# Layer 0's projections: two sequences without a zero column between them, token mixing in instructions of 640 columns, all of it on VectorE

## The chip, the cores and the metric

The kernel runs on one core of a Trainium2 chip. The metric is the device time of one execution in microseconds (us). Five engines work side by side, each on its own list of instructions, in order: TensorE (PE for its products, PEld for its loading of stationary operands), VectorE (DVE), ScalarE (ACT), GpSimd (POOL) and SyncE (SP), which here only starts transfers. They wait for each other through semaphores.

## The reference, cut to what matters

One step of a trunk of two layers runs over 512 latent tokens and 128 context tokens, 1024 features each. Layer 0 mixes tokens with a recurrence in both directions. Its inputs come from a token shift:

```python
def centred_token_shift(x):
    zero = jnp.zeros_like(x[:, :1])
    prev = jnp.concatenate([zero, x[:, :-1]], axis=1)
    nxt = jnp.concatenate([x[:, 1:], zero], axis=1)
    return 0.5 * (prev + nxt)

delta = centred_token_shift(h) - h                      # h: modulated norm of x
xs = h[None] + delta[None] * mu[:, None, None, :]       # six mixed inputs
r, k, v = xs[0] @ w_r, xs[1] @ w_k, xs[2] @ w_v         # xs[3..5]: low-rank maps w, a, g
```

Neither sequence sees the other one: the first and the last token of each have a zero as their missing neighbour. The recurrence (the scan), the projection back, an MLP, layer 1's attention and its MLP follow.

## The kernel before, in words

Features lie on the 128 partitions, in 8 tiles (k = 0 to 7), and tokens along the columns: 512 latent, then 128 context, 640 in all. Products are made exact in float32 by splitting each factor into a rounded part and a rest, `xh` and `xl` for an input, `whi` and `wlo` for weights, and by three products of each pair of tiles, in two halves of 320 columns (`fm_step`, L205).

`start_norm` makes the modulated norm. `xt` is x divided by its rms (L434); `hp` (L447, ScalarE) is scale and shift of it, 644 columns wide: a zero, 512 latent columns, two zeros, 128 context columns, a zero. `n_s` (L450) is the sum of both neighbours of each column in one instruction of 642 columns, and `dl` (L452) is half of it less `hp`, one instruction for each sequence. The odd tiles of L434 and the even tiles of L450 run on GpSimd.

`phase_proj` makes the six mixed inputs. `mix(m, k)` writes a tile `mixt` of 640 columns with two instructions on VectorE (L477, 512 and 128 columns, since `hp` has zeros between the sequences) and hands it to `split`: ScalarE rounds it to `xh` (L247), and the rest `xl` (L248) is made on GpSimd, for k = 0 and 4 on VectorE. That is 48 mixes, 36 of them with `xl` on GpSimd. Two `mixt` buffers turn, 8 buffers hold `xh` and `xl` of an input that a whole product reads, and two more those of a low-rank step.

The order of the phase: the low-rank map of the decay (m = 3), with its second stage (`l2lo` L539, `l2x` L533, products L548 and L550, ScalarE L553); the mixes of m = 1, then for eight pieces the product of k and one step of the next low-rank map (m = 4); the mixes of m = 0, then for eight pieces the product of r, a step of the last map (m = 5) and all that r, k and a give, written to DRAM (L601 to L622; GpSimd adds and multiplies in L623 and L624); the mixes of m = 2 beside the gate (`l2x` L646 and L647, product, L652 and L653). Then v's product and the scan start, whose first loads are queued behind the last of these steps.

The program is written in this order, and a scheduler at build time, which works from estimated costs, sets the order on each engine. A change of instructions in one place can so shift others, in later phases too.

Of the kernel before, what the change touches and what calls it, by code (L numbers as in the profile page):

```python
# [28 lines left out]
# ---------------------------------------------------------------- host layout  # L29
# [16 lines left out]
def _constants():  # L46
# [18 lines left out]
    # masks of the chunk products: rows (b | k), columns (at | rt), one per direction  # L65
# [43 lines left out]
def _tmaj(v):  # L109
    """[1024] of (ph, pp, hp, v) -> [(hp, pp, t), (ph, v)]"""  # L110
    a = np.asarray(v).reshape(4, 2, 2, 64).transpose(2, 1, 0, 3).reshape(4, 1, 256)
    return np.broadcast_to(a, (4, 32, 256)).reshape(P, 256)


def _bias(rpb):
    """Relative position bias of every query against its key band, -1e30 outside of the window:
    [head, query (g, r, j), kind of column block, key (g, r, j)]."""
# [54 lines left out]
# ---------------------------------------------------------------- device  # L172
class K:
# [11 lines left out]
    # -- weights: 128 columns of a [1024, n] matrix -> exact float32r pair  # L185
# [10 lines left out]
    # -- feature-major product of one 128-column piece: two PSUM tiles [128, 320]  # L196
# [3 lines left out]
    def fm_step(self, ps, w, x, k, n):  # L200
        """Columns 0 .. 319 and the others: tokens and whatever columns follow them."""
        N = x[0].shape[-1]
        for j, (a, b) in enumerate(((w[0], x[0]), (w[0], x[1]), (w[1], x[0]))):
            for g, (c, e) in enumerate(((0, HALF), (HALF, N))):
                self.nc.tensor.matmul(ps[g][:, :e - c], lhsT=a[:, k, :], rhs=b[:, c:e],  # L205
                                      start=(k == 0 and j == 0), stop=(k == n - 1 and j == 2))
# [7 lines left out]
    # -- token-major product, 256 columns at a time; out(t, b, psum)  # L214
# [36 lines left out]
    # -- y = x ** -0.5 on VectorE  # L251
# [14 lines left out]
    # -- adaLN vectors  # L266
# [12 lines left out]
    def ada_first(self, l, blk, pool, pa, mm=None):  # L279
        """Columns 256 * blk .. + 256 of layer l's adaLN, summed over four rows each."""  # L280
# [11 lines left out]
    def ada_second(self, l, blk, sb, pm, mm=None):  # L292
        """... and on into mods[l][:, 2 * blk : 2 * blk + 2, :]."""
# [8 lines left out]
    def gscale(self, l, s, pool):  # L302
        """norm_g * (1 + scale) -> [128, 8, 2]"""
# [21 lines left out]
    # -- 1/rms of every token, on all partitions: [128, 640]  # L325
# [14 lines left out]
    def ssq(self, k):  # L340
        """Feature tile k of the residual is complete: its squares into the running sum."""
# [8 lines left out]
    def rms_first(self, acc, pool):  # L350
        """-> 1/rms, token-major."""
# [12 lines left out]
    def rms_second(self, rs, pool):  # L364
        """... on all partitions."""
# [13 lines left out]
    # ------------------------------------------------------------------  # L379
    def run(self):  # L380
        nc, tc = self.nc, self.tc
        with ExitStack() as st:
# [6 lines left out]
            # per 128 tokens and four head pairs: kk, r; per direction kd, bp; decay exponents  # L389
# [28 lines left out]
    def start_norm(self, st, hp, dl):  # L418
        """hp: modulated norm of x with a zero around each sequence; dl: what the token shift adds."""
# [10 lines left out]
        nc.vector.memset(hp[:, :, 513:515], 0.0)  # L430
        nc.vector.memset(hp[:, :, 643:644], 0.0)
        rb = self.rms_bcast(xt, p2)
        for k in range(KT):
            (nc.gpsimd if k % 2 else nc.vector).tensor_tensor(xt[:, k, :], xt[:, k, :], rb, op=ALU.mult)  # L434
        gs = self.const.tile([P, 8, 2], F32, name="gs00")
        m = self.mods[0]
        for j in range(4):
# [7 lines left out]
            for k in range(2 * j, 2 * j + 2):  # L445
                for o, a, c, i in ((1, 0, TS, 0), (515, TS, TP, 1)):
                    nc.scalar.activation(hp[:, k, o:o + c], xt[:, k, a:a + c], AF.Identity, scale=gs[:, k, i:i + 1],  # L447
                                         bias=m[:, k, i:i + 1])
                s = p2.tile([P, 642], F32, name="n_s")
                (nc.vector if k % 2 else nc.gpsimd).tensor_tensor(s, hp[:, k, 0:642], hp[:, k, 2:644], op=ALU.add)  # L450
                for (a, b, c) in ((0, 0, TS), (TS, 514, TP)):
                    nc.vector.scalar_tensor_tensor(dl[:, k, a:a + c], s[:, b:b + c], 0.5,  # L452
                                                   hp[:, k, b + 1:b + 1 + c], op0=ALU.mult, op1=ALU.subtract)

    def phase_proj(self, sc):
        nc, tc = self.nc, self.tc
        with ExitStack() as st:
# [5 lines left out]
            hp = hpool.tile([P, KT, 644], F32, name="hp")  # L463
# [10 lines left out]
            def mix(m, k):  # L474
                t = mp.tile([P, T], F32, name="mixt")
                for (a, b, c) in ((0, 1, TS), (TS, 515, TP)):
                    nc.vector.scalar_tensor_tensor(t[:, a:a + c], dl[:, k, a:a + c], mu[:, m * 8 + k:m * 8 + k + 1],  # L477
                                                   hp[:, k, b:b + c], op0=ALU.mult, op1=ALU.add)
                return self.split(xq if m != 2 and k % 4 == 3 else xp, t, lo_eng=nc.gpsimd if k % 4 else nc.vector)
# [23 lines left out]
            class Lora1:  # L503
                """First stage of a low-rank map, one feature tile at a time."""
# [20 lines left out]
            def lora2(lw, j):  # L525
                """Second stage of the low-rank maps: stacked exact pairs."""
# [39 lines left out]
            # k and the decay exponents  # L566
# [21 lines left out]
            # r, and all that r, k and a give  # L588
# [55 lines left out]
            # gate  # L644
# [13 lines left out]
            # v, token-major, while the scan's first step is prepared  # L658
# [12 lines left out]
    # -- sums over the features of every head: [32 * (token tile) + head, token], the prompt's in columns 128 .. 255  # L671
# [14 lines left out]
    def head_tokens(self, y, psm):  # L686
        """... token-major: [token, 32 * (token tile) + head]."""
# [5 lines left out]
    def head_bcast(self, pool, y):  # L693
        """What a product needs to bring per-head factors to all features: rows twice, exact pair."""
# [14 lines left out]
    # ------------------------------------------------------------------  # L709
    def c_slots(self, pool, n, par):  # L710
        """Tiles of a window: [16 (z, e, q), at | rt], half identities, [8 (e, q), b | k time-major]."""
# [5 lines left out]
    def scan_pools(self, st):  # L717
# [9 lines left out]
        # state and chunk values [z, pp, ph, v]: head half z has G on partition half z, (U | V) on the other  # L727
# [4 lines left out]
        # window tiles of even and odd steps  # L732
# [99 lines left out]
    def mm(self, *a, op=None, **k):  # L832
        """Matmul issued behind the previous one of this kind."""
# [15 lines left out]
    def start_sample(self, d):  # L849
        """The given state into the next tile of direction d."""  # L850
# [14 lines left out]
    def fill(self, n):  # L865
        """Emit up to n groups of chunk products of coming units, as far as there is room."""
# [15 lines left out]
    def prep_elem(self, ts, hg, d, i):  # L882
        """Decays of a unit (four head pairs, one direction, a window of 64 tokens) and the scaled r, k, kk, b."""
# [47 lines left out]
    def prep_group(self, ts, hg, d, i, e):  # L931
        """Chunk products and time-major copies, eight (head, chunk) at a time."""
# [28 lines left out]
    def invert(self, ts):  # L961
        """(I - N)^-1 of all 32x32 blocks of a step in place, one block per partition."""
# [20 lines left out]
    def chain_step(self, ts, n, e, d):  # L983
        """One chunk of one direction in four stages: R, U, state, Y."""
# [7 lines left out]
        if n == 1 and e == 0:  # L992
            # the tile that holds the prompt's last state is written out, the sample starts in the other one
# [63 lines left out]
    def state_update(self, ts, n, e, d, gu, nx, C):  # L1057
        """G of the next chunk: accumulated in PSUM within a window, copied to the tile of the next chunk."""
# [6 lines left out]
        if e == 0 and n < 2:  # L1065
            # a new window: its first G is in SBUF only
# [29 lines left out]
    def post_half(self, tt, hb, on_dve):  # L1096
        """Group norm, bonus and gate of 64 tokens; o goes out feature-major."""
# [52 lines left out]
    def residual(self, out, k, ps, gate, x):  # L1150
        """out = x + gate * product, for feature tile k (both PSUM tiles)."""
# [5 lines left out]
    def late_pools(self):  # L1157
        """The odd steps' tiles make room for the output projection."""
# [411 lines left out]
```

## Time and profile before

| | us |
|---|---|
| median of three runs (2279.73 to 2282.37) | 2279.94 |
| span of the profiled execution, first to last instruction | 2277.6 |
| PE busy in the span | 2022.0 |
| PEld / DVE / ACT / POOL busy | 1836.7 / 1198.3 / 866.0 / 544.3 |

The page gives no time of the profiled execution besides its span; the median of the runs is 2.3 us above it. The page cuts the span into 40 slices of 57 us. In the first 6 slices, in which layer 0's projections lie (from about 28 to 322 us), PE is busy for 5 to 9 tenths with the granted clock at 5 to 9 tenths of full speed, and DVE for 6 to 8 tenths. From slice 17 on PE is busy for 9 tenths and more at full clock. A share of busy time is an average over stretches with different limits; it is read by stretch.

### The profile page before, as it was taken

The numbers are of one execution on the slowest core, as the hardware profiler recorded it, in microseconds if no ns is written. First come the engines' busy times: TensorE is split into PE (matmuls) and PEld (weight loads), VectorE is DVE, ScalarE is ACT, GpSimd is POOL, SyncE is SP. The second block draws the span as 40 slices with busy tenths as digits, with TensorE's granted clock in tenths as the row PEclk, the third lists the DMA queues.
The fourth block names the chain that finished last, engine by engine and source line by source line (L and its number), as shares of the span: only waits on it lengthen the run. The fifth ranks groups of instructions, "written<-read, shape, count | busy, mean of one in ns | idle before, by whom it ended". The sixth has DMA issues, their size and how long they took to land.

```text
span 2277.6 us, 44909 instructions
## 1 busy us (share of the span) xinstructions
PE 2022.0 (89%) x18516; PEld 1836.7 (81%) x18516; DVE 1198.3 (53%) x2593; ACT 866.0 (38%) x1734; POOL 544.3 (24%) x602
## 2 busy tenths in 40 slices
PE   5898978875567567999999999999999999999999
PEld 2687867754456457899999999888777999999999
DVE  6838574676886865433333335334566643434342
ACT  3435454355454334322232233222476431313130
POOL 2404368465552143101010010000132110101010
PEclk8597979988788788899999999999899999999999
DMA  6344855454443454322222323443411232222221
GB/s 229 103 131 131 252 186 163 127 165 141 139 138 117 106 165 136 122 93 93 93 86 91 93 75 94 142 129 94 138 43 32 78 120 75 75 75 75 75 75 73
DMA packets 161388, 260.01 MB, mean 114 GB/s; under 512 B 46880, under 2 KB 103328, under 8 KB 161184
## 3 DMA queue, kind: packets, MB, share of 16 engines
q1 hardware_dynamic: 146816, 240.37, 33.9%
q10 hardware_dynamic: 14368, 16.78, 2.2%
q8 instruction: 145, 2.38, 0.4%
q14 instruction: 59, 0.48, 0.1%
HBM read 218.18 MB, written 37.35 MB: 112 GB/s over the span
## 4 chain that ended last, share of the span: by engine, by line
PE 64%; DVE 11%; DMA 4%; POOL 3%; ACT 2%; issue 2%; SPq 1%; ACTq 0%; DVEq 0%; POOLq 0%
PE psl L205 48%; PE psl L239 3%; DVE invX L978 2%; PE ps L1497 2%; DVE invT L975 2%; POOL C L929 2%; PE po L1534 2%; PE pp L834 2%; PE pt L1522 2%; DVE C L959 1%; PE pp L1201 1%; PE psl L286 1%; PE A L834 1%; DMA ld_s<-scr 1%; PE psl L1238 1%
## 5 line engine op out<-in xcount | busy, mean ns | idle before, releaser
L191 ACT CAST whi<-wraw 128x1024 fp32r<-128x1024 f32 x179 | 187.2, 1048 | 727.6 <-PE psl L205 696.3
L205 PE MATMUL psl<-xh,whi 128*128 128x320 f32 (+1 forms) x1712 | 422.4, 320 | 20.1 <-ACT whi L191 14.5
L205 PE MATMUL psl<-xl,whi 128*128 128x320 f32 (+1 forms) x1712 | 419.1, 318 | 10.3 <-POOL xl L248 5.4
L205 PE MATMUL psl<-xh,wlo 128*128 128x320 f32 (+1 forms) x1712 | 415.7, 316 | 2.2 <-DVE wlo L193 2.2
L205 PEld LDWEIGHTS psl<-xh,whi 128*128 128x128 f32 x1712 | 297.2, 193 | 40.8 <-ACT whi L191 18.8
L205 PEld LDWEIGHTS psl<-xl,whi 128*128 128x128 f32 x1712 | 297.4, 193 | 18.2 <-POOL xl L248 7.5
L205 PEld LDWEIGHTS psl<-xh,wlo 128*128 128x128 f32 x1712 | 298.6, 193 | 4.6 <-DVE wlo L193 2.6
L1317 POOL TENSOR_TENSOR relu<-relu 128x640 f32<-128x640 f32 x64 | 80.6, 1261 | 753.5 <-ACT relu L1316 748.8
L1154 DVE SCALAR_TENSOR_TENSOR xres<-psl,mods,xres 128x320 f32<-128x320 f32 (+2 forms) x216 | 81.7, 434 | 305.5 <-PE psl L205 305.5
L205 PE MATMUL psl<-hhh,wlo 128*128 128x320 f32 x1024 | 233.4, 309 | 0.0
L205 PE MATMUL psl<-hhl,whi 128*128 128x320 f32 x1024 | 233.3, 309 | 0.0
L205 PE MATMUL psl<-hhh,whi 128*128 128x320 f32 x1024 | 233.2, 309 | 0.0
L193 DVE TENSOR_TENSOR wlo<-wraw,whi 128x1024 fp32r<-128x1024 f32 x179 | 222.6, 1246 | 9.6 <-ACT whi L191 9.2
L205 PEld LDWEIGHTS psl<-hhh,whi 128*128 128x128 f32 x1024 | 171.2, 188 | 0.4 <-issue 0.4
L205 PEld LDWEIGHTS psl<-hhh,wlo 128*128 128x128 f32 x1024 | 171.2, 188 | 0.0
L205 PEld LDWEIGHTS psl<-hhl,whi 128*128 128x128 f32 x1024 | 171.1, 188 | 0.0
L834 PE MATMUL pp<-C,KB 128*64 128x128 f32 x1280 | 103.3, 313 | 41.3 <-DVE C L959 17.6
L1274 DVE TENSOR_TENSOR relu<-psl,rms_b 128x320 f32<-128x320 f32 x128 | 60.8, 486 | 144.7 <-PE psl L205 143.6
L834 PEld LDWEIGHTS pp<-C,KB 128*64 128x64 f32 x1280 | 85.8, 158 | 54.2 <-issue 26.7
L248 DVE TENSOR_TENSOR hhl<-relu,hhh 128x640 fp32r<-128x640 f32 x64 | 53.4, 834 | 127.3 <-ACT hhh L247 127.2
L248 POOL TENSOR_TENSOR xl<-mixt,xh 128x640 fp32r<-128x640 f32 x36 | 67.3, 1873 | 135.6 <-ACT xh L247 126.6
L959 DVE TENSOR_TENSOR C<-pp,cstsb 64x512 f32<-64x512 f32 x80 | 55.0, 688 | 83.0 <-ACT C L956 69.2
(291 smaller groups left out, 3480.7 us busy)
## 6 DMA issues: line engine op xcount, KB each, us to landing
wraw<-in_mlp_w SPq DMA_DIRECT2D x128, 512.0 KB, 3.5
adaraw<-in_ada_w SPq DMA_DIRECT2D x96, 512.0 KB, 4.9
ld_d<-scr SPq DMA_DIRECT2D x20, 512.0 KB, 4.3
ld_s<-scr SPq DMA_DIRECT2D x20, 512.0 KB, 3.8
bias<-in_bias SPq DMA_DIRECT2D x16, 384.0 KB, 3.6
scr<-ta SPq DMA_DIRECT2D x16, 325.0 KB, 3.4
wi<-scr SPq DMA_DIRECT2D x20, 260.0 KB, 4.5
scr<-bp SPq DMA_DIRECT2D x16, 320.0 KB, 4.2
```

What stands on the lines that cost most here:

```text
L191: nc.scalar.copy(hi, raw)
L193: nc.vector.tensor_tensor(lo, raw, hi.bitcast(F32), op=ALU.subtract)
L205: self.nc.tensor.matmul(ps[g][:, :e - c], lhsT=a[:, k, :], rhs=b[:, c:e], start=(k == 0 and j == 0), stop=(k == n - 1 and j == 2))
L239: nc.tensor.matmul(ps, lhsT=a[:, tc_], rhs=w, start=(k == 0 and j == 0), stop=(k == KT - 1 and j == 2))
L248: (lo_eng or nc.vector).tensor_tensor(xl, src, xh.bitcast(F32), op=ALU.subtract)
L834: r = (op or self.nc.tensor.matmul)(*a, **k)
L929: nc.gpsimd.tensor_tensor(rev(o) if s == 0 else o, v4(sh, s, ww)[hs], f[hs], op=ALU.mult)
L959: nc.vector.tensor_tensor(C[o, 8 * h:8 * h + 8, :], pn[o, :, 0:64], mask[o], op=ALU.mult)
L975: nc.vector.tensor_tensor(t, X[:, s + 1:, s:s + 1].broadcast_to([P, m, b - a]), X[:, s:s + 1, a:b].broadcast_to([P, m, b - a]), op=ALU.mult)
L1154: nc.vector.scalar_tensor_tensor(out[:, a:b], ps[g][:, o:o + b - a], gate[:, k, j:j + 1], x[:, a:b], op0=ALU.mult, op1=ALU.add)
L1274: nc.vector.tensor_tensor(t[:, c], ps[q][:, :HALF], rb[:, c], op=ALU.mult)
L1317: nc.gpsimd.tensor_tensor(t, t, t, op=ALU.mult)
```

## The change: what it does

`hp` gets 642 columns: a zero, 512 latent columns, 128 context columns, a zero. The two sequences lie side by side. The neighbour sum `n_s` is one instruction of 640 columns, wrong in the two columns at the seam, and a new copy of two elements (L451 of the changed kernel) puts the right sums there. `dl` is one instruction of 640 columns instead of two, and so is each mix (L475). All of `xt`, `n_s` and `xl` goes to VectorE. GpSimd keeps the two operations of each of the eight pieces of r (L621 and L622). The other lines of the diff drop comments; line numbers after `start_norm` shift by one or two.

```diff
-        nc.vector.memset(hp[:, :, 513:515], 0.0)
-        nc.vector.memset(hp[:, :, 643:644], 0.0)
+        nc.vector.memset(hp[:, :, T + 1:T + 2], 0.0)
-            (nc.gpsimd if k % 2 else nc.vector).tensor_tensor(xt[:, k, :], xt[:, k, :], rb, op=ALU.mult)
+            nc.vector.tensor_tensor(xt[:, k, :], xt[:, k, :], rb, op=ALU.mult)
-                for o, a, c, i in ((1, 0, TS, 0), (515, TS, TP, 1)):
-                    nc.scalar.activation(hp[:, k, o:o + c], xt[:, k, a:a + c], AF.Identity, scale=gs[:, k, i:i + 1],
+                for a, c, i in ((0, TS, 0), (TS, TP, 1)):
+                    nc.scalar.activation(hp[:, k, a + 1:a + 1 + c], xt[:, k, a:a + c], AF.Identity, scale=gs[:, k, i:i + 1],
-                s = p2.tile([P, 642], F32, name="n_s")
-                (nc.vector if k % 2 else nc.gpsimd).tensor_tensor(s, hp[:, k, 0:642], hp[:, k, 2:644], op=ALU.add)
-                for (a, b, c) in ((0, 0, TS), (TS, 514, TP)):
-                    nc.vector.scalar_tensor_tensor(dl[:, k, a:a + c], s[:, b:b + c], 0.5,
-                                                   hp[:, k, b + 1:b + 1 + c], op0=ALU.mult, op1=ALU.subtract)
+                s = p2.tile([P, T], F32, name="n_s")
+                nc.vector.tensor_tensor(s, hp[:, k, 0:T], hp[:, k, 2:T + 2], op=ALU.add)
+                nc.vector.tensor_copy(s[:, TS - 1:TS + 1], hp[:, k, TS - 1:TS + 3:3])
+                nc.vector.scalar_tensor_tensor(dl[:, k], s, 0.5, hp[:, k, 1:T + 1], op0=ALU.mult, op1=ALU.subtract)
-            hp = hpool.tile([P, KT, 644], F32, name="hp")
+            hp = hpool.tile([P, KT, T + 2], F32, name="hp")
-                for (a, b, c) in ((0, 1, TS), (TS, 515, TP)):
-                    nc.vector.scalar_tensor_tensor(t[:, a:a + c], dl[:, k, a:a + c], mu[:, m * 8 + k:m * 8 + k + 1],
-                                                   hp[:, k, b:b + c], op0=ALU.mult, op1=ALU.add)
-                return self.split(xq if m != 2 and k % 4 == 3 else xp, t, lo_eng=nc.gpsimd if k % 4 else nc.vector)
+                nc.vector.scalar_tensor_tensor(t, dl[:, k], mu[:, m * 8 + k:m * 8 + k + 1], hp[:, k, 1:T + 1],
+                                               op0=ALU.mult, op1=ALU.add)
+                return self.split(xq if m != 2 and k % 4 == 3 else xp, t)
```

The first place where the order changes is VectorE at the start of the first low-rank map, right behind the last `dl`. Numbers behind a name count buffers. Before, seven rows hold two mixes in two parts each and one `xl`:

```order
L248 TENSOR_TENSOR xl_430<-mixt_426,xh_429 128x640
L477 SCALAR_TENSOR_TENSOR mixt_452<-dl_69,parsb_58,hp_68 128x512
L477 SCALAR_TENSOR_TENSOR mixt_452<-dl_69,parsb_58,hp_68 128x128
L477 SCALAR_TENSOR_TENSOR mixt_465<-dl_69,parsb_58,hp_68 128x512
L477 SCALAR_TENSOR_TENSOR mixt_465<-dl_69,parsb_58,hp_68 128x128
L193 TENSOR_TENSOR wlo_422<-wraw_418,whi_420 128x1024
L539 TENSOR_TENSOR l2lo_533<-wraw_537,l2w0_540 64x1024
```

In the changed kernel, at the same place:

```order
L248 TENSOR_TENSOR xl_428<-mixt_425,xh_427 128x640
L248 TENSOR_TENSOR xl_440<-mixt_437,xh_439 128x640
L475 SCALAR_TENSOR_TENSOR mixt_449<-dl_69,parsb_58,hp_68 128x640
L475 SCALAR_TENSOR_TENSOR mixt_461<-dl_69,parsb_58,hp_68 128x640
L193 TENSOR_TENSOR wlo_421<-wraw_417,whi_419 128x1024
L248 TENSOR_TENSOR xl_452<-mixt_449,xh_451 128x640
L248 TENSOR_TENSOR xl_464<-mixt_461,xh_463 128x640
```

Every rest `xl` now stands in VectorE's own list, mostly one mix behind its own.

The second place is GpSimd's list from its first work of the phase. Before:

```order
L434 TENSOR_TENSOR xt_79<-xt_79,rms_b_147 128x640 x4
L450 TENSOR_TENSOR n_s_215<-hp_68 128x642
L450 TENSOR_TENSOR n_s_264<-hp_68 128x642
L450 TENSOR_TENSOR n_s_313<-hp_68 128x642
L450 TENSOR_TENSOR n_s_362<-hp_68 128x642
L248 TENSOR_TENSOR xl_443<-mixt_439,xh_442 128x640
L248 TENSOR_TENSOR xl_456<-mixt_452,xh_455 128x640
```

In the changed kernel its first work is that of the first pieces of r:

```order
L621 TENSOR_TENSOR ke_1493<-ta0_1495,ta1_1496 128x640
L622 TENSOR_TENSOR ke_1493<-ke_1493,r_1565 128x640
L621 TENSOR_TENSOR ke_1662<-ta0_1664,ta1_1665 128x640
L622 TENSOR_TENSOR ke_1662<-ke_1662,r_1734 128x640
L621 TENSOR_TENSOR ke_1781<-ta0_1783,ta1_1784 128x640
```

44 instructions have left GpSimd: 4 `xt`, 4 `n_s` and 36 `xl`.

The third place is VectorE at the turn from the pieces of r to the gate, up to the rest of the gate's input, `l2x1`. Before:

```order
L641 TENSOR_TENSOR l2w1_2553<-wraw_2549,l2w0_2551 128x1024
L477 SCALAR_TENSOR_TENSOR mixt_2562<-dl_69,parsb_58,hp_68 128x512
L477 SCALAR_TENSOR_TENSOR mixt_2562<-dl_69,parsb_58,hp_68 128x128
L618 SCALAR_TENSOR_TENSOR bp_2523<-ta1_2419,ksq_2501 128x640
L477 SCALAR_TENSOR_TENSOR mixt_2569<-dl_69,parsb_58,hp_68 128x512
L477 SCALAR_TENSOR_TENSOR mixt_2569<-dl_69,parsb_58,hp_68 128x128
L522 TENSOR_SCALAR lw_2545<-lw_2545 128x640
L621 SCALAR_TENSOR_TENSOR ta1_2419<-ta1_2419,ke_2416 128x640
L477 SCALAR_TENSOR_TENSOR mixt_2576<-dl_69,parsb_58,hp_68 128x512
L477 SCALAR_TENSOR_TENSOR mixt_2576<-dl_69,parsb_58,hp_68 128x128
L647 TENSOR_TENSOR l2x1_2613<-lw_2545,l2x0_2612 128x640
```

In the changed kernel:

```order
L639 TENSOR_TENSOR l2w1_2512<-wraw_2508,l2w0_2510 128x1024
L619 SCALAR_TENSOR_TENSOR ta0_2378<-ta0_2378,ke_2376 128x640
L475 SCALAR_TENSOR_TENSOR mixt_2532<-dl_69,parsb_58,hp_68 128x640
L520 TENSOR_SCALAR lw_2504<-lw_2504 128x640
L616 SCALAR_TENSOR_TENSOR bp_2482<-ta1_2379,ksq_2460 128x640
L248 TENSOR_TENSOR xl_2529<-mixt_2526,xh_2528 128x640
L248 TENSOR_TENSOR xl_2535<-mixt_2532,xh_2534 128x640
L645 TENSOR_TENSOR l2x1_2564<-lw_2504,l2x0_2563 128x640
```

Between the rest of the gate's weights and `l2x1` one mix and two rests stand now, where three mixes in two parts each stood.

## Rows read from the trace of the kernel before

**Rows 1.** Stretches: length; busy PE, PEld, DVE, ACT, POOL; PEclk, DMA share, GB/s.

```profile
28.00:84.00 56.00, 33.20 (x152) 22.71 (x153) 48.21 (x66) 26.42 (x43) 31.34 (x16) 0.63 0.38 114
84.00:106.00 22.00, 22.00 (x60) 15.52 (x59) 17.30 (x28) 9.82 (x18) 7.84 (x5) 0.50 0.26 79
106.00:180.00 74.00, 74.00 (x477) 64.09 (x476) 31.04 (x57) 29.25 (x52) 8.14 (x5) 0.97 0.44 133
180.00:216.00 36.00, 31.22 (x124) 23.55 (x123) 32.40 (x44) 20.23 (x36) 14.86 (x8) 0.67 0.34 97
216.00:245.00 29.00, 25.02 (x151) 22.51 (x150) 24.24 (x30) 12.46 (x19) 13.47 (x9) 0.88 0.82 237
245.00:299.00 54.00, 53.52 (x344) 45.34 (x344) 30.66 (x35) 26.93 (x46) 19.17 (x12) 1.00 0.78 231
299.00:322.00 23.00, 12.39 (x63) 10.51 (x61) 22.22 (x30) 10.63 (x21) 12.74 (x8) 0.70 0.48 153
```

**Rows 2.** Timeline of 100 to 135 us: start, duration, engine, line, count, idle before.

```profile
99.02 1.89 POOL L248 TENSOR_TENSOR xl<-mixt,xh 128x640 fp32r<-128x640 f32 x1 [1.96 <-ACT xh L247]
99.43 1.63 DVE L477 SCALAR_TENSOR_TENSOR mixt<-dl,parsb,hp 128x128 f32<-128x128 f32 x1
...
102.62 1.01 DVE L477 SCALAR_TENSOR_TENSOR mixt<-dl,parsb,hp 128x512 f32<-128x512 f32 x2
...
103.56 0.81 DVE L248 TENSOR_TENSOR xl<-mixt,xh 128x640 fp32r<-128x640 f32 x1
```

**Rows 3.** Instructions of lines 248, 618 and 300: durations in ns, least/median/most.

```profile
L248 POOL TENSOR_TENSOR xl<-mixt,xh x36: 1532/1702/3762, 52.8 to 321.5; 128x640 fp32r<-128x640 f32 x36
...
L618 DVE SCALAR_TENSOR_TENSOR bp<-ta,ksq x16: 810/826/2179, 219.8 to 301.9; 128x640 f32<-128x640 f32 x16
...
L300 DVE TENSOR_TENSOR mods<-adp,parsb x8: 148/162/164, 21.2 to 44.2; 128x4 f32<-128x4 f32 x8
```

**Rows 4.** Groups on DVE from 28 to 84 us: busy us, mean ns, idle before.

```profile
L477 DVE SCALAR_TENSOR_TENSOR mixt<-dl,parsb,hp 128x512 f32<-128x512 f32 x12 | 13.8, 1153 | 3.0 <-POOL xl L248 2.9
L434 DVE TENSOR_TENSOR xt<-xt,rms_b 128x640 f32<-128x640 f32 x4 | 7.1, 1829 | 1.6 <-ACT rms_b L376 1.6
L452 DVE SCALAR_TENSOR_TENSOR dl<-n_s,hp 128x512 f32<-128x512 f32 x8 | 6.9, 856 | 0.0
L450 DVE TENSOR_TENSOR n_s<-hp 128x642 f32<-128x642 f32 x4 | 6.6, 1647 | 0.2
...
L477 DVE SCALAR_TENSOR_TENSOR mixt<-dl,parsb,hp 128x128 f32<-128x128 f32 x11 | 3.8, 343 | 0.0
L452 DVE SCALAR_TENSOR_TENSOR dl<-n_s,hp 128x128 f32<-128x128 f32 x8 | 3.3, 412 | 0.0
```

**Rows 5.** Timeline of DVE at the turn from k to r.

```profile
181.71 2.32 DVE L477 SCALAR_TENSOR_TENSOR mixt<-dl,parsb,hp 128x512 f32<-128x512 f32 x2
183.95 1.21 DVE L539 TENSOR_TENSOR l2lo<-wraw,l2w 64x1024 fp32r<-64x1024 f32 x1
188.85 2.46 DVE L539 TENSOR_TENSOR l2lo<-wraw,l2w 64x1024 fp32r<-64x1024 f32 x1
...
192.72 2.91 DVE L533 TENSOR_TENSOR l2x<-lw,l2x 64x640 fp32r<-64x640 f32 x2
```

**Rows 6.** Waits of PE from 216 to 245 us: total us, times, longest.

```profile
PE psl L611 <- DVE ksq L612: 2.8, 1, 2.8
```

**Rows 7.** Groups on DVE from 286 to 323 us.

```profile
L477 DVE SCALAR_TENSOR_TENSOR mixt<-dl,parsb,hp 128x512 f32<-128x512 f32 x9 | 10.1, 1124 | 1.8 <-POOL xl L248 1.8
L477 DVE SCALAR_TENSOR_TENSOR mixt<-dl,parsb,hp 128x128 f32<-128x128 f32 x9 | 9.6, 1061 | 0.0
```

**Rows 8.** Waits of PE from 299 to 323 us.

```profile
PE psl L205 <- ACT l2x L646: 7.0, 1, 7.0
```

**Rows 9.** Waits of all engines from 28 to 345 us.

```profile
POOL xl L248 <- ACT xh L247: 126.6, 28, 40.7
...
PE psl L205 <- ACT whi L191: 6.4, 1, 6.4
```

## The prediction, made before the run

> **What bounds the kernel now.** The first view is the table of busy time by stretch. The reader is to see in it where TensorE has no gap and where VectorE has none [rows 1]. From 84 to 180 us PE is busy all the time (22.00 of 22.00, 74.00 of 74.00), from 245 to 299 almost all (53.52 of 54). What VectorE or GpSimd save there cannot be given back by PE at once. In the other stretches PE stands still: 22.8 of 56 us before 84, 4.8 of 36 from 180 to 216, 4.0 of 29 from 216 to 245, 10.6 of 23 from 299 to 322. There VectorE is the fullest engine: 48.21, 32.40, 24.24 and 22.22 us. In them the granted clock is also lower (0.63, 0.67, 0.88, 0.70) than in 106 to 180 (0.97).
>
> The second view is the timeline of a quiet place in the dense stretch. A 128-column mix, started beside a GpSimd rest, takes 1.63 us and ends at 101.06, when GpSimd's instruction, 1.89 us from 99.02, has ended at 100.91; the pair of 512 and 128 columns alone takes 1.01 [rows 2]. VectorE with two inputs and GpSimd with two inputs stretch each other. The groups say the same: nine mixes of 128 columns take 1061 ns each late in the phase, eleven early on 343 [rows 4, 7]. Where four `xt` ran on VectorE beside four on GpSimd, one took 1829 ns [rows 4]; an undisturbed instruction of 640 columns with two inputs takes 826 [rows 3].
>
> The third view is the waits. PE waits 2.8 us for `ksq` of VectorE [rows 6], 7.0 us for the gate's `l2x` [rows 8], which hangs on VectorE's list through `lw` (L522), and 6.4 us for the first weights `whi` of ScalarE [rows 9]. GpSimd waits 126.6 us in 28 waits for the cast `xh`, at no price to others [rows 9].
>
> **The change part by part.** Prices: a mix, `dl`, `xt` or `n_s` of 640 columns 0.82 to 0.83 us (median of L618) [rows 3], a rest 0.81 [rows 2], the copy of two elements 0.16, as a tiny instruction of L300 [rows 3]. A pair beside a GpSimd rest takes 2.32 us, alone 1.01 [rows 2, 5], so a collision costs VectorE 1.3, more than the 0.81 it pays for doing the rest itself. Joining the pair saves 1.01 − 0.83 = 0.18 more, in 48 mixes 8.6 us, though only what falls into stretches that VectorE bounds comes to the end.
>
> 28 to 84. Before, VectorE spends 13.8 + 3.8 on mixes, 7.1 on `xt`, 6.9 + 3.3 on `dl`, 6.6 on `n_s` [rows 4] and 3 × 0.81 on its own rests: 43.9 us, and waits 2.9 for GpSimd's rest. Afterwards: 8 `xt`, 8 `n_s`, 8 `dl`, 24 × 0.82 = 19.7; 12 mixes × 0.83 = 10.0; 11 rests × 0.81 = 8.9; 8 copies × 0.16 = 1.3; in all 39.9. That is 4.0 less, and the 2.9 of waits go; the copies and the eight more rests are in it. Late next are the modulation vectors (L300, up to 44.2 [rows 3]), whose transfers this change does not hasten: I estimate 1.5 of new waiting. That leaves 5.4. Part of PE's idle is the 6.4 for `whi` [rows 9], which no edit here moves. If this ends last, the gain is 0; at most it is 7. I take 4, near the sum.
>
> 84 to 180. Taken at 0: PE hides it. VectorE goes ahead, and the gain of the stretch before is handed on.
>
> 180 to 216. Two pairs beside GpSimd at about 2.32 become 0.83 each: the collision part is 2 × 1.31. One `l2lo` of 2.46 becomes 1.21, its undisturbed time next to it; two `l2x` of 2.91 together become 2 × 0.82 [rows 5]. Three mixes are joined, 3 × 0.18. Two rests come in, 2 × 0.81. Sum: 2.6 + 1.25 + 1.27 + 0.5 − 1.6 = 4.0. PE's idle there is 4.8, and it runs at half clock behind it; bounds 1 and 8; I take 4.
>
> 216 to 245. `ksq`, for which PE waited 2.8 [rows 6], comes earlier where mixes shrink, but the DMA share is 0.82 [rows 1], so transfers may take the place. Bounds 0 and 6 (4.0 of idle and as much by the clock); I take 3.
>
> 245 to 299: 0, PE has half a microsecond of idle.
>
> 286 to 322. Nine mixes cost 10.1 + 9.6 = 19.7 [rows 7]; afterwards 9 × 0.83 = 7.5, and nine rests 7.3: 4.9 less, and the 1.8 of waiting for GpSimd goes. The sum is 6.7, against a wait of PE of 7.0 [rows 8]. The chain to it runs from PE's last step through `lw` to ScalarE's `l2x`, and of the nine mixes only those ahead of `lw` stand on it; the part behind `lw` helps the last piece's outputs and the scan's first loads. Bounds 1 and 7; I take 4.5.
>
> After 322 the scan follows in a chain through several engines, and passes a shift on. The scheduler changes some order there too; no row prices this; I take 0, with 3 to either side.
>
> The new waits: VectorE takes its list in order, so a rest waits there for ScalarE's cast, with weight rests, mixes and evictions queued behind. In the new order 37 of 48 rests stand at least one mix behind their own, 11 directly behind it. The mix between them covers the cast; the 11 are in my ranges.
>
> Sum: 4 + 4 + 3 + 4.5 = 15.5. The profiled span, 2277.6, becomes 2262.1; the median of the runs is 2.3 above the span, so 2264.4.
>
> The row of 1.63 us shows a VectorE instruction that ends when GpSimd's does [rows 2]. The Trainium skill, "SBUF — State Buffer", section "SBUF: two separate sides", says that both engines share one pair of ports, and that whoever has it holds it for the whole instruction while the other blocks fully. The trace agrees. By that rule a collision could cost as much as a rest of GpSimd lasts, 1.53 at least [rows 3], instead of 1.3, and the sum would be 15.5 × 1.53 / 1.3 = 18, the time 2262.
>
> **The rivals.** First, a larger gain. From 84 to 106 PE works without a gap at a clock of 0.50, then at 0.97 [rows 1]. If the denser start before it lets the full clock begin earlier, the 22 us shrink until VectorE bounds them: 17.3 less five collisions (5 × 1.46 with the joining) plus five rests (5 × 0.81) is 14. That is 8 more: 2256. Against it: the clock stayed at 0.50 through 22 us without a gap, and the work of PE ahead of it remains loose.
>
> Second, the gain is swallowed: `whi` (6.4) ends the first stretch's wait, transfers hold 216 to 245 (share 0.82), the chain to `l2x` is PE's and ScalarE's. With every term at its low end, 0 + 1 + 0 + 1 = 2, the time is 2278, and 2281 with the scan's 3. For it: VectorE's idle before its mixes was small, but PE's waits name ScalarE twice. Against it: behind `l2x` stands a list of VectorE full of stretched mixes.
>
> Third, slower: VectorE becomes the bound by waiting for casts. About 19 rests (8, 2 and 9) move to it in the stretches it fills. GpSimd waited 1.96 us for such a cast in the row shown [rows 2]. When a moved rest waits 15.5 / 19 = 0.8 us on average, the gain is gone; from there on it is a loss. At half of 1.96 each, 18.6 in all, the time is 2283; weight rests `wlo` and evictions queued behind would then also tear gaps into 84 to 180. For it: ScalarE has other work, 20.23 of 36 us at the turn [rows 1]. Against it: most rests have a mix of 0.83 us between.
>
> That the change doesn't do what it says I exclude: GpSimd's list has lost its 44 instructions in the order.
>
> **How the numbers follow.** The forecast, 2258 to 2271 (6 to 7 us to either side, which the scan's 3 and two terms at their ends fill), has a chance of 0.62. The larger gain has 0.11, the swallowed one 0.17 (0.05 of it still faster, 0.12 the same), the loss 0.10. The measurement tells 0.2% from no change, 4.6 us here, so "the same" is 2275.4 to 2284.5; the third rival, beyond that when evictions are held up too, is counted as slower. Together: faster 0.62 + 0.11 + 0.05 = 0.78, same 0.12, slower 0.10. The range that should hold the time 8 times in 10 is the forecast's, with most of the larger gain and half of the swallowed one: 2252 to 2278.
>
> **What would show it right or wrong.** In the profile after, GpSimd has no `xt`, `n_s` or `xl`; mixes last 0.83, rests 0.81; `l2lo` is back at 1.21 everywhere. PE becomes dense about 4 us before 84, the turn's second `l2x` comes about 8 us before 195.6, the gate's wait shrinks from 7.0 to about 3, and v's product and the scan start 15 us sooner. VectorE's waits for `xh` stay below some 10 us in all. It is wrong if those waits are large; if PE's start hangs on `whi` as before; if 84 to 106 runs at another clock; or if what is won by 322 us is lost in the scan.

## The result, and the profile after

The changed kernel takes 2248.74 us, median of four runs (2246.10 to 2253.26), the kernel before 2280.12. The ratio on record is 0.9867, with a 95% interval of 0.9851 to 0.9883. The forecast was 2264.4, the range 2252 to 2278: the direction was right, the gain is 31.4 us where 15.5 were forecast. The profiled execution has a span of 2248.5 us, 29.1 less than before.

The stretches of the changed kernel, in the columns of [rows 1]:

```profile
28.00:84.00 56.00, 38.92 (x175) 27.70 (x173) 49.29 (x79) 29.73 (x50) 0.00 (x0) 0.88 0.38 115
84.00:106.00 22.00, 22.00 (x135) 18.40 (x134) 18.15 (x32) 12.90 (x23) 0.00 (x0) 1.00 0.48 144
106.00:180.00 74.00, 70.59 (x440) 58.88 (x440) 36.76 (x61) 32.98 (x56) 0.00 (x0) 0.95 0.49 149
180.00:216.00 36.00, 32.91 (x131) 27.05 (x130) 26.50 (x40) 16.80 (x30) 3.13 (x2) 0.67 0.30 92
216.00:245.00 29.00, 28.76 (x192) 24.84 (x191) 15.58 (x20) 13.90 (x23) 9.43 (x6) 1.00 0.98 289
```

The line to look at is the second. Before, PE was busy for all 22 us with 60 products at a granted clock of 0.50 [rows 1]; now it is busy just as long with 135 at 1.00. A full busy column said nothing of the work done in it.

Four instructions mark the end of each part: the first product of the low-rank map's second stage, the head sums of k (`kkv`, L587 before, L585 after), the head sums of r (L627, L625), and the first product with `hhh`, the MLP behind the scan. They are shown here first before, then after (count; least, median and most duration in ns; first and last start in us):

```profile
L548 PE MATMUL st<-l2x,l2w x64: 303/309/634, 84.6 to 296.8; 128*128 128x320 f32 x64
L587 DVE TENSOR_SCALAR kkv<-pk x1: 405/405/405, 187.3 to 187.3; 128x256 f32<-128x256 f32 x1
L627 DVE COPY kkv<-pk x1: 411/411/411, 320.6 to 320.6; 128x256 f32<-128x256 f32 x1
L205 PE MATMUL psl<-hhh,whi x1024: 305/309/412, 982.3 to 2272.4; 128*128 128x320 f32 x171
```

```profile
L546 PE MATMUL st<-l2x,l2w x64: 303/309/634, 80.2 to 281.5; 128*128 128x320 f32 x64
L585 DVE TENSOR_SCALAR kkv<-pk x1: 410/410/410, 171.0 to 171.0; 128x256 f32<-128x256 f32 x1
L625 DVE COPY kkv<-pk x1: 406/406/406, 297.9 to 297.9; 128x256 f32<-128x256 f32 x1
L205 PE MATMUL psl<-hhh,whi x1024: 305/309/412, 953.3 to 2243.4; 128*128 128x320 f32 x171
```

From these rows, by first starts: the first stage ends 4.4 us earlier, k takes 90.8 us instead of 102.7 (11.9 less), k's end to r's end 126.9 instead of 133.3 (6.4 less), r's end to the MLP 655.4 instead of 661.7 (6.3 less), and from there to the last product with `hhh` it is 1290.1 in both. 4.4 + 11.9 + 6.4 + 6.3 = 29.0.

VectorE's groups in 28 to 84 us after (busy, mean ns, idle before) answer to [rows 4]:

```profile
L475 DVE SCALAR_TENSOR_TENSOR mixt<-dl,parsb,hp 128x640 f32<-128x640 f32 x14 | 12.2, 879 | 0.1
L248 DVE TENSOR_TENSOR xl<-mixt,xh 128x640 fp32r<-128x640 f32 x13 | 10.4, 817 | 0.0
L449 DVE TENSOR_TENSOR n_s<-hp 128x640 f32<-128x640 f32 x8 | 6.3, 816 | 0.0
L433 DVE TENSOR_TENSOR xt<-xt,rms_b 128x640 f32<-128x640 f32 x8 | 6.0, 818 | 1.6 <-ACT rms_b L376 1.6
L451 DVE COPY n_s<-hp 128x2 f32<-128x2 f32 x8 | 1.1, 162 | 0.0
```

The prices were right: 0.82 for `xt` and `n_s`, 0.82 for a rest, 0.16 for the copy; a mix took 0.88 where 0.83 was forecast. In the same 56 us VectorE now does 14 mixes and 13 rests, where it had done 12 mixes [rows 4] and 3 rests.

### The profile page after: what moved, and what is told of

Same layout as the page of the kernel before. It is cut to its first block, busy times and chain, and to the rows that moved or that the text cites. A ratio compares the mean times of both kernels' runs of the same rounds, so it can differ in the third digit from the quotient of the medians.

```text
span 2248.5 us, 44838 instructions
## 1 busy us (share of the span) xinstructions
PE 2007.7 (89%) x18516; PEld 1823.6 (81%) x18516; DVE 1180.0 (52%) x2587; ACT 866.0 (39%) x1735; POOL 463.8 (21%) x558
## 4 chain that ended last, share of the span: by engine, by line
PE 73%; DVE 13%; DMA 6%; ACT 3%; POOL 2%; issue 2%; SPq 1%; ACTq 0%; DVEq 0%; POOLq 0%
PE psl L205 53%; PE psl L239 4%; PE ps L1495 2%; DVE invT L973 2%; DVE invX L976 2%; PE po L1532 2%; PE pp L832 2%; POOL C L927 2%; PE pt L1520 2%; DVE C L957 1%; PE psl L286 1%; DMA ld_s<-scr 1%; PE pp L1199 1%; DMA wi<-scr 1%; PE st L548 1%
## 5 line engine op out<-in xcount | busy, mean ns | idle before, releaser
L832 PE MATMUL pp<-C,KB 128*64 128x128 f32 x1280 | 97.6, 298 | 27.2 <-DVE C L957 13.1
L832 PEld LDWEIGHTS pp<-C,KB 128*64 128x64 f32 x1280 | 79.9, 149 | 41.3 <-issue 20.7
L1032 ACT ACTIVATE GU<-A 32x256 f32<-32x256 f32 x160 | 60.0, 375 | 84.3 <-DVE mods L300 51.8
```

The source lines that it names most:

```text
L832: r = (op or self.nc.tensor.matmul)(*a, **k)
L1032: nc.scalar.activation(gu[64 - 64 * hp:96 - 64 * hp, hp, pp].rearrange("p b v -> p (b v)"), U[32 * q:32 * q + 32, :], AF.Copy, scale=-0.5)
```

## The experiments

All times are medians. The experiments ran in three batches, each with the kernel before beside it: 2279.23 us (11 runs), 2277.23 (17) and again 2277.23 (22), 2268.06 to 2284.03 in all; a difference across batches is uncertain by some 2 us. The first of them holds c_same, e_xl_pool, e_mix_two and e_ghost, the second e_norm_pool and the three fills, the third the rest. The last four columns are read off the same four instructions in one profile of each kernel, "k takes" from the first to the second, and so on. The ratio, as recorded, is to the kernel before.

| kernel | runs, us | ratio (95%) | first stage ends | k takes | r and gate | to the MLP |
|---|---|---|---|---|---|---|
| before | 2277.2 to 2279.2 | | 84.6 | 102.7 | 133.3 | 661.7 |
| changed | 2248.7 | 0.9867 (0.9851, 0.9883) | 80.2 | 90.8 | 126.9 | 655.4 |
| c_same, changed again | 2247.6 | 0.9869 (0.9849, 0.9889) | 77.7 | 90.8 | 127.2 | 661.8 |
| e_norm_pool | 2252.1 | 0.9891 (0.9870, 0.9912) | 78.0 | 90.3 | 128.4 | 660.7 |
| e_mix_two (profiled run 2264.2) | 2255.7 | 0.9905 (0.9876, 0.9933) | 80.7 | 105.4 | 123.7 | 659.0 |
| e_mix_two_b | 2247.7, one run | | 77.5 | 91.9 | 126.8 | 654.2 |
| e_mix_two_c | 2265.8, one run | | 77.9 | 106.3 | 124.4 | 659.8 |
| e_xl_pool | 2269.0 | 0.9957 (0.9942, 0.9973) | 77.5 | 106.0 | 128.4 | 658.4 |
| e_pool_all | 2268.1 | 0.9961 (0.9948, 0.9973) | 82.9 | 96.2 | 132.0 | 658.0 |
| e_ghost | 2295.2 | 1.0074 (1.0060, 1.0088) | 87.0 | 103.2 | 138.5 | 667.9 |
| e_ghost_xh | 2283.5 | 1.0025 (1.0009, 1.0040) | 84.2 | 103.4 | 135.8 | 654.3 |
| e_before_fill | 2273.1 | 1.0000 (0.9979, 1.0022) | 84.6 | 96.3 | 131.7 | 663.1 |
| e_fill_first | 2256.8 | 0.9908 (0.9890, 0.9927) | 77.3 | 103.1 | 122.8 | 654.7 |
| e_fill_turn | 2249.4 | 0.9877 (0.9859, 0.9895) | 79.9 | 90.6 | 120.4 | 660.9 |

Theories. A: VectorE's collisions with GpSimd are the main thing, and the granted clock at the first pieces of k follows from what they do to TensorE. B: fewer instructions on VectorE are the gain. C: the new order is. D: the clock has nothing to do with it.

**The changed kernel again (c_same).** No edit.

> The changed kernel once more, beside the others on the same chip. It took 2246.1 to 2253.3 us in four runs, a wider spread than the kernel before (2279.7 to 2282.4). If TensorE's granted clock at the first pieces of k (80 to 106 us) is what the surplus over the forecast came from, this profile too shows them at full speed, with the last k step near 171 us; a run in which they went at half speed would end about 10 us later, so that single runs fall into two groups. If the surplus is only less work on VectorE, the runs scatter around one value and the k step ends at the same time whatever the clock was.

Measured: 2244.67 to 2254.86 in four runs, k in 90.8 us, full clock from 80 us on. No run of the eight (four here, four in the first result) fell to the 2260s. Between these two executions of one program the start of the second stage differs by 2.5 us (80.2 and 77.7) and the last column of the table by 6.4, so differences of that size, the 6.3 from before to after among them, cannot be told from chance.

**Rests on GpSimd again (e_xl_pool).**

```diff
-                return self.split(xq if m != 2 and k % 4 == 3 else xp, t)
+                return self.split(xq if m != 2 and k % 4 == 3 else xp, t, lo_eng=nc.gpsimd if k % 4 else nc.vector)
```

> The changed kernel with one thing undone: the rests xl of the tiles with k not 0 or 4 are made on GpSimd again (36 of 48); the joined instructions of 640 columns, and xt and n_s on VectorE, stay. Theory A (the collisions of VectorE with GpSimd are the main thing, and the clock follows from the gaps they tear into TensorE): the mixes beside a rest of GpSimd last about 1.6 to 2 us again, the second l2x of the first map comes 3 us or more later than 79 us, the first pieces of k run at half clock again, and the time is 2268 to 2275. Theory B (what counts is that there are fewer instructions on VectorE): 2249 to 2254. Theory C (the new order counts, not what is slow): no telling stretch by stretch, anything.

2269.04: theory A's value, against B. But one detail failed: the first stage ended no later (77.5), and still k ran at half clock (106.0 us). PE in two stretches of 4 us (length, busy and count, clock, DMA share, GB/s):

```profile
84.00:88.00 4.00, 4.00 (x12) 0.50 0.28 83
104.00:108.00 4.00, 4.00 (x16) 0.50 0.28 83
```

Against c_same, k takes 15.2 us more and the other three columns together 2.4 less. So in this profile the rests on GpSimd cost what they cost nearly all by the clock.

**Mixes in two instructions again (e_mix_two, three profiles).**

```diff
-                nc.vector.scalar_tensor_tensor(t, dl[:, k], mu[:, m * 8 + k:m * 8 + k + 1], hp[:, k, 1:T + 1],
-                                               op0=ALU.mult, op1=ALU.add)
+                for a, c in ((0, TS), (TS, TP)):
+                    nc.vector.scalar_tensor_tensor(t[:, a:a + c], dl[:, k, a:a + c], mu[:, m * 8 + k:m * 8 + k + 1],
+                                                   hp[:, k, a + 1:a + 1 + c], op0=ALU.mult, op1=ALU.add)
```

> The changed kernel with one thing undone: each mix is two instructions again, of 512 and of 128 columns; all rests, xt and n_s stay on VectorE. It costs 0.18 us a mix. Theory A: some 20 mixes stand in the stretches that VectorE bounds, so 3.6 us, and 2252 to 2255; if the later start takes the full clock from the first pieces of k, up to 2264. Theory B (fewer instructions): more than half of what was won is lost, 2265 or more.

The runs lay in two groups: 2248.24, 2248.35, 2249.99 and 2261.39, 2264.18, 2268.20. The profiled one was of the upper. So the same kernel was profiled twice more.

> The kernel with each mix in two instructions once more, unchanged, for a second profile. Its six runs lay in two groups, 2248.2 to 2250.0 and 2261.4 to 2268.2, and the profiled one (2264.2) had the first pieces of k at half clock, its last k step at 186.1 us. Theory A (the clock of that stretch alone divides the groups): a run near 2249 has those pieces at full clock and its last k step at 171 to 174, with VectorE's instructions as long as in the first profile; a run near 2264 looks like the first. If a run near 2249 shows half clock there too, theory A is wrong.

> The same kernel a third time, with the same expectation: near 2249 with full clock from the first pieces of k and the last k step at 171 to 174 us, or near 2264 with half clock there and the last k step at about 186.

The two profiles show one run of each kind. Stretches of 4 us on PE, first of the run of 2247.7, then of 2265.8:

```profile
72.00:76.00 4.00, 3.35 (x12) 0.62 0.04 15
76.00:80.00 4.00, 3.28 (x14) 1.00 0.46 131
84.00:88.00 4.00, 4.00 (x18) 1.00 0.62 185
100.00:104.00 4.00, 4.00 (x27) 1.00 0.52 163
```

```profile
72.00:76.00 4.00, 2.74 (x12) 0.87 0.05 19
76.00:80.00 4.00, 3.40 (x11) 0.55 0.42 131
84.00:88.00 4.00, 4.00 (x11) 0.50 0.28 83
100.00:104.00 4.00, 4.00 (x12) 0.50 0.28 83
```

The work up to there is the same, and the second stage starts at 77.5 and 77.9 us. From then on one has the full clock and the other the half, and k ends at 169.4 and 184.2, both some 2 us earlier than expected:

```profile
L586 DVE TENSOR_SCALAR kkv<-pk x1: 410/410/410, 169.4 to 169.4; 128x256 f32<-128x256 f32 x1
```

```profile
L586 DVE TENSOR_SCALAR kkv<-pk x1: 410/410/410, 184.2 to 184.2; 128x256 f32<-128x256 f32 x1
```

This is the cleanest comparison of all: one program, 14.4 us in k (91.9 and 106.3), and only the clock differs where it starts. The spans differ by 18.0; of the rest, 2.4 come back between k and r, and 5.6 lie behind r's end, within what one program varies there. That something comes back is seen in all three profiles at half clock with the rests on VectorE (e_mix_two, e_mix_two_c and, below, e_fill_first): 122.8 to 124.4 us from k to r, where c_same, e_norm_pool and e_mix_two_b at full clock took 126.8 to 128.4.

At full clock, joining the mixes brings nothing once the rests are on VectorE: 2247.7 with two instructions a mix, 2247.6 in the changed kernel. What it may bring is the full clock itself: with two instructions a mix 4 of 8 runs were in the upper group, with one none of 8. Eight runs of each are too few to be sure.

**Spare rests on GpSimd (e_ghost, e_ghost_xh).** The first reads what a rest reads, the second `xh` twice.

```diff
+                xh, xl = self.split(xq if m != 2 and k % 4 == 3 else xp, t)
+                if k % 4:
+                    nc.gpsimd.tensor_tensor(gh, t, xh.bitcast(F32), op=ALU.subtract)
+                return xh, xl
...
+            gh = l2.tile([P, T], F32, name="gh")
```

> The changed kernel with GpSimd doing the 36 rests of tiles with k not 0 or 4 a second time, into a tile that nothing reads. Nobody waits for their result, so only their being there (a collision with VectorE, and that they hold a mixt buffer longer) can cost. Theory A: about 28 of them meet a VectorE instruction with two inputs and cost it up to 1.3 us each; in the stretches that VectorE bounds some 19 x 0.7 to 1.3 us = 13 to 25 us, with the clock's part on top: 2262 to 2280. Theory B (fewer instructions on VectorE): under 2 us, 2249 to 2251. Theory C (the order): the same as B as long as VectorE's order stays nearly the same.

> The changed kernel with 36 spare instructions of 640 columns on GpSimd as in the ghost experiment, but reading xh twice instead of mixt and xh, so that they hold no mixt buffer. If the collision with VectorE is what cost 47 us there, this costs nearly as much, 2285 to 2297. If it was the two mixt buffers, held until GpSimd was done, it falls to 2250 to 2260.

Work whose result nobody reads costs 47.5 us over the changed kernel's 2247.6, more than the whole change had won, and more than I expected (2262 to 2280). Without a hold on the `mixt` buffers it still costs 35.8; 2283.5 lies just under the 2285 to 2297 that I expected. So about three quarters are the collision and what follows from it, the rest the buffers. The clock is in both: k took 103.2 and 103.4 us, as at half clock. (The profiled run of e_ghost_xh, in the table, was the quickest of its twelve, 2272.91; most lay above 2281.) VectorE's groups from 28 to 330 us, in the changed kernel and in e_ghost:

```profile
L475 DVE SCALAR_TENSOR_TENSOR mixt<-dl,parsb,hp 128x640 f32<-128x640 f32 x48 | 43.0, 903 | 0.3
L248 DVE TENSOR_TENSOR xl<-mixt,xh 128x640 fp32r<-128x640 f32 x48 | 41.5, 877 | 5.0 <-ACT xh L247 4.8
L193 DVE TENSOR_TENSOR wlo<-wraw,whi 128x1024 fp32r<-128x1024 f32 x19 | 25.2, 1327 | 8.5 <-ACT whi L191 8.4
```

```profile
L248 DVE TENSOR_TENSOR xl<-mixt,xh 128x640 fp32r<-128x640 f32 x44 | 52.9, 1209 | 8.4 <-ACT xh L247 8.2
L475 DVE SCALAR_TENSOR_TENSOR mixt<-dl,parsb,hp 128x640 f32<-128x640 f32 x46 | 51.1, 1117 | 6.1 <-POOL gh L479 5.9
L193 DVE TENSOR_TENSOR wlo<-wraw,whi 128x1024 fp32r<-128x1024 f32 x19 | 30.3, 1592 | 1.5 <-ACT whi L191 1.3
```

Each rest is 332 ns longer, each mix 214, each weight rest 265. VectorE also waits 5.9 us for the spare instruction to let a buffer go. In e_ghost_xh nothing waits for a buffer, and rests take 1122 ns, mixes 1179.

How an instruction gets longer is seen in the order of time, here in e_ghost (start, duration):

```profile
70.62 1.68 POOL L479 TENSOR_TENSOR gh<-mixt,xh 128x640 f32<-128x640 f32 x1 [3.11 <-ACT xh L247]
70.78 2.20 DVE L475 SCALAR_TENSOR_TENSOR mixt<-dl,parsb,hp 128x640 f32<-128x640 f32 x1
73.89 2.39 POOL L479 TENSOR_TENSOR gh<-mixt,xh 128x640 f32<-128x640 f32 x1 [1.59 <-ACT xh L247]
74.78 2.18 DVE L475 SCALAR_TENSOR_TENSOR mixt<-dl,parsb,hp 128x640 f32<-128x640 f32 x1
```

Both mixes begin while GpSimd works and end 0.68 us behind it (72.98 against 72.30, 76.96 against 76.28). From 28 to 330 us 7 mixes begin so, and all end 0.68 or 0.69 us behind; of 20 rests 13 do, and the others keep their 0.81. In e_ghost_xh it is 15 mixes of 15. In the kernel before all 11 pieces of 512 columns that begin under a GpSimd instruction end 0.54 or 0.55 us behind it, all 13 of 128 columns 0.15. So the instruction does most of its work when GpSimd is through: a collision costs VectorE nearly what is left of GpSimd's instruction.

**Norm work on GpSimd again (e_norm_pool).** `xt` of odd and `n_s` of even tiles.

```diff
+            (nc.gpsimd if k % 2 else nc.vector).tensor_tensor(xt[:, k, :], xt[:, k, :], rb, op=ALU.mult)
+                (nc.vector if k % 2 else nc.gpsimd).tensor_tensor(s, hp[:, k, 0:T], hp[:, k, 2:T + 2], op=ALU.add)
```

> The changed kernel with xt of the odd tiles and the neighbour sums of the even tiles on GpSimd again; all rests stay on VectorE. In the kernel before four xt on VectorE took 7.1 us beside four on GpSimd, eight alone cost 6.6, the neighbour sums the same: so VectorE gains under 2 us by having GpSimd's share too. Expected: the first product of the first map within 2 us of the changed kernel's, and 2247 to 2252 if the first pieces of k keep the full clock, about 2260 if they lose it. If instead the moved norm work is what made the start earlier, its first product of the second stage comes 3 us or more later than 80 us.

2252.12, at the edge of the expectation. First stage (78.0 against 77.7) and k (90.3 against 90.8) are as in c_same. The time is 4.5 us above c_same's, but the intervals of the two ratios overlap: what moving the norm's work is worth lies between nothing and some 5 us here.

**Both on GpSimd again: the joined instructions alone (e_pool_all).** The edits of e_xl_pool and e_norm_pool together.

> The changed kernel's layout and its joined instructions of 640 columns alone: rests, xt and neighbour sums are shared with GpSimd as in the kernel before. With the rests alone on GpSimd it was 2269; norm work on GpSimd cost about 4 more on VectorE's side. Theory A: 2268 to 2276, the first pieces of k at half clock. Theory B (fewer instructions on VectorE are the gain): 2250 to 2258.

2268.14, the same as e_xl_pool, by another way: the first stage ends 5.4 us later (82.9 against 77.5), but the full clock comes at about 93 us, and k takes 96.2 instead of 106.0. So beside rests on GpSimd the norm's work does delay the start in this profile. The joined layout alone brings 9 us; 48 times 0.18 would be 8.6, if all of it came to the end. Before and in e_pool_all, from 28 to 330 us:

```profile
L477 DVE SCALAR_TENSOR_TENSOR mixt<-dl,parsb,hp 128x512 f32<-128x512 f32 x48 | 49.6, 1035 | 10.1 <-POOL xl L248 9.8
L477 DVE SCALAR_TENSOR_TENSOR mixt<-dl,parsb,hp 128x128 f32<-128x128 f32 x48 | 33.4, 695 | 0.0
```

```profile
L475 DVE SCALAR_TENSOR_TENSOR mixt<-dl,parsb,hp 128x640 f32<-128x640 f32 x48 | 54.0, 1140 | 7.1 <-POOL xl L248 6.8
```

A mix of two pieces took 1035 + 695 = 1730 ns, one of a single piece takes 1140 with GpSimd just as busy. In the kernel before 21 of 48 mixes began a piece under a GpSimd instruction: 8 the first, 10 the second, 3 both. In e_pool_all 11 of 48 did. The second piece is one more place where GpSimd can get ahead.

**More products in the first map (e_before_fill on the kernel before, e_fill_first on the changed one).**

```diff
+            def filler(n, w, x):
+                ft = pst.tile([P, 512], F32, name="st0")[:, :HALF]
+                for i in range(n):
+                    nc.tensor.matmul(ft, lhsT=w, rhs=x[:, :HALF], start=True, stop=True)
...
+                    if fill:
+                        filler(fill, s_.w[0][:, k, :], x[0])
...
-                lora.step(k)
+                lora.step(k, 6 if k > 1 else 0)
```

> The kernel before, with 36 products more in the first low-rank map (six for each of the tiles k = 2 to 7, repeats of the product of xh and whi into a PSUM tile that nothing reads), so that TensorE has work while it waits for the rest xl. Nothing on VectorE, ScalarE or GpSimd is changed. Theory A (the granted clock at the first pieces of k follows from the gaps ahead of it): the full clock comes well before 110 us, the last k step earlier than 187 us although there is more to compute, and the time is 2262 to 2272, 8 to 17 us under the kernel before. Theory D (the clock has nothing to do with the gaps; the changed kernel's surplus came from VectorE alone): the fill costs up to 3 us, 2279 to 2283.

> The changed kernel with the same 36 products more in its first low-rank map. It already has the full clock at the first pieces of k in its profiles, so theory A expects no gain in the best runs, but fewer runs above 2250: median 2244 to 2249. Theory D: 0 to 3 us slower.

Both missed. On the kernel before, seven runs lay at 2267.59 to 2273.55 and five at 2281.84 to 2289.42; the mean shows no difference. In the profiled run, of the lower group, the full clock came at about 94 us instead of 110, and k took 96.3 instead of 102.7. On the changed kernel the fill made it 2256.78: the first map now ran at full clock from 60 to 75 us, fell to half at 76, and k took 103.1. So products in gaps move the clock's fall and rise, but not where one wants them.

**Products at the turn from k to r (e_fill_turn).**

```diff
+                if j:
+                    filler(9, lw)
```

Here `filler` multiplies `lw` by a constant; the trace has 18 instructions for the nine products.

> The changed kernel with nine products more, of the low-rank map's result lw with a constant, into a PSUM tile that nothing reads, at the turn from k to r, where TensorE stands still for 3 us (171.4 to 174.8) and then runs at half clock up to about 196 us. Theory A: if the gap is what takes the clock away, the half clock shrinks or goes, the k-to-gate stretch gets up to 10 us shorter, and the time is 2238 to 2245. Theory D: 0 to 2 us slower than the changed kernel, 2248 to 2251.

The clock did what theory A said. PE in 4 us stretches, in the changed kernel and with the fill:

```profile
172.00:176.00 4.00, 1.28 (x5) 0.66 0.40 125
176.00:180.00 4.00, 3.65 (x11) 0.50 0.28 94
184.00:188.00 4.00, 4.00 (x13) 0.50 0.01 4
```

```profile
172.00:176.00 4.00, 4.00 (x17) 1.00 0.36 125
176.00:180.00 4.00, 4.00 (x20) 1.00 0.23 68
184.00:188.00 4.00, 4.00 (x22) 1.00 0.00 0
```

The part up to r's end shrank from 126.9 to 120.4 us. The time did not: 2249.44 (2246.71 to 2251.29). Of the 6.5 us nothing is to be seen at the end, and why is open; behind r's end one program varies by as much. It is not a version that beats the changed kernel.

## Why the prediction was wrong, point by point

- The step that failed is "84 to 180. Taken at 0: PE hides it." k took 11.9 us less. I took a PE without gaps as a bound that nothing on other engines could move, though the row showed it at half clock [rows 1]. This was my first rival, with a chance of 0.11 and a price of 8 us, and one of the signs of being wrong that I named ("if 84 to 106 runs at another clock"). The price was low as well: I let the half clock end at 106 us, while PE was still at 0.50 up to 108, and bounded the gain by VectorE. In its place the runs show the granted clock: full from about 80 us on instead of from 110, which e_mix_two_b and e_mix_two_c price at 14.4 us in k. PE before:

```profile
104.00:108.00 4.00, 4.00 (x13) 0.50 0.20 58
108.00:112.00 4.00, 4.00 (x22) 0.70 0.51 165
```

  The page before has VectorE at 3 to 8 tenths in its first six slices, 3 in the third (114 to 171 us), not at 6 to 8: it does not fill the whole of this stretch.
- 28 to 84, forecast 4: it was 4.4, in c_same 6.9. `whi` is still waited for (7.1 us, [rows 9] had 6.4), but it did not eat the gain. The moves did not add up as the sum had it: with the norm's work back on GpSimd the first stage ends at 78.0, with the rests back at 77.5, with both at 82.9, so by these single profiles either move alone brings it. One program varies by 2.5 to 3.2 us there.
- The turn, 216 to 245 and 286 to 322, forecast 4 + 3 + 4.5 = 11.5: they brought 6.4. From k's end to the second `l2x` it is 2.2, forecast 4, since PE still waits there, 2.7 us, now for ScalarE's cast (first row). PE's wait for the gate's `l2x` fell from 7.0 [rows 8] to 4.5, not to 3 (second):

```profile
PE psl L205 <- ACT xh L247: 2.7, 1, 2.7
```

```profile
PE psl L205 <- ACT l2x L644: 4.5, 1, 4.5
```

- After 322, taken at 0, "with 3 to either side": 6.3 less in the profile, 0.1 more in the second profile of the same kernel. The bound should have been 6; the value is not refuted. As far as the two profiles tell, the 6.3 are luck.
- The collision, 1.3 us each: right in kind, but no fixed price; it is nearly what is left of GpSimd's instruction. That "joining the pair saves 1.01 − 0.83 = 0.18" was the price without GpSimd; beside it the saving is 0.59 (1730 to 1140 ns). The Trainium skill ("SBUF — State Buffer", "SBUF: two separate sides") says that of the two engines the one that comes second blocks fully; the mixes that end 0.68 us behind GpSimd, all 15 of 15 in e_ghost_xh, agree. The 2262 that the prediction drew from this rule does not account for the surplus either, since the clock does not stand in that sum.
- The new wait, VectorE for the cast `xh`, forecast below some 10 us: 4.8. The third rival did not happen.
- The second rival, a gain swallowed by other waits, did not happen: the first stage and the turn gave 10.8 us between them.

Theory A stands in its first half: e_ghost and e_ghost_xh (collision without any change of VectorE's own work) show it, and e_xl_pool and e_pool_all show that rests on GpSimd cost some 20 us, in e_xl_pool nearly all by the clock. Its second half, that the clock follows from the gaps, is only partly shown: the clock is what divides the groups, but e_xl_pool had an early first stage and half clock, and more products did not fetch it. What tips it stays open. PE's busy time just ahead does not tell: from 72 to 80 us it was 6.63 in e_mix_two_b and 6.04 in e_fill_turn, which got the full clock, and 6.39 in e_mix_two, which did not. The Trainium skill ("TensorE: Matmul & The Clock Gate", "Part 1: The HAM clock gate (the "warmup" mystery)") says that the rate follows how busy PE has been recently; these runs neither show nor refute it. Theory D falls with e_mix_two_b and e_mix_two_c. Theory B, as the whole cause, falls with e_xl_pool and e_mix_two_b. Theory C was not tested alone, so how much of the gain is due to the new order is not shown.

## What to carry to other kernels

A stretch in which TensorE is always busy is not bounded by its work as long as its clock is at half: count its products per microsecond, and price a rival at the whole stretch of low clock, less what the stretch behind it gives back. GpSimd beside a full VectorE is no free help: ask what each of its instructions costs the other engine, and beside it split nothing on VectorE that can be one piece. Where runs fall into two groups, profile one of each before explaining the mean.

## What the hardware showed that I had not expected

- One program, with the same start of a dense stretch (77.5 and 77.9 us), ran it at either clock: 91.9 or 106.3 us for k, 2247.7 or 2265.8 in all.
- 36 spare instructions on a GpSimd that has only 16 others in these projections cost 47.5 us of 2248.
- The collision is not confined to instructions with two inputs. VectorE's one-input instruction of 128x256 at L258 took 294 ns in the changed kernel and 1620 in e_pool_all, where it ends 0.15 us behind a rest of GpSimd:

```profile
179.98 1.69 POOL L248 TENSOR_TENSOR xl<-mixt,xh 128x640 fp32r<-128x640 f32 x1 [1.52 <-ACT xh L247]
180.20 1.62 DVE L258 TENSOR_SCALAR rsq_i<-kkv 128x256 int32<-128x256 int32 x1
```

- VectorE's instructions with an input in PSUM were not held up: nine `ksq` (L614 of e_ghost, one of its inputs the product `psl`) begin while GpSimd works and keep their 0.53 to 0.55 us.
